# Scores of the RWKV key pair: masked copy on VectorE against a plain copy on ScalarE and a select on GpSimd

## The chip, the cores and the metric

The kernel runs on one core of a Trainium2 chip. The time is the device time of one execution in microseconds (us), and smaller is better. Engines carry the names of the profile: PE is TensorE (PEld its weight load), DVE VectorE, ACT ScalarE, POOL GpSimd, SP SyncE. A pair of an engine and a line, as DVE L542, means that engine's instructions of line 542 of the kernel before.

## The reference

A trunk of two layers over 256 tokens of width 1024. In each layer the normed input goes through one input projection into four token mixers (stick-breaking attention, RWKV-7 time mixing, MoBA attention, HGRN2 recurrence) and four gates; the gated sum of the four branches goes through an output projection, and an FFN of inner width 2816 follows. The part that matters here is RWKV's recurrence:

```python
def step(state, inp):
    r_t, w_t, k_t, v_t, a_t, b_t = inp
    sa = jnp.einsum('bhvk,bhk->bhv', state, a_t)
    state = (state * w_t[:, :, None, :] + sa[..., None] * b_t[:, :, None, :]
             + v_t[..., None] * k_t[:, :, None, :])
    return state, jnp.einsum('bhvk,bhk->bhv', state, r_t)
```

It runs over 256 steps in 4 heads of 64. A chunked form replaces the steps by products of matrices: for each chunk of 128 steps and each head there is a 128x128 score of every step s against every later step t, once for the pair (b, a) and (b, r), once for (k, a) and (k, r). Scores against a count where s < t, scores against r where s <= t, and all others are zero.

## The kernel before

All matrix products run on PE. A weight arrives as a raw tile of 128x1024 by a DMA on SP's queue, ACT rounds it into `hi` (L128) and DVE takes the rest as `lo = raw - hi` (L129); three matmuls then stand for one product (`mm3`). There are four buffers each for `raw`, `hi` and `lo`, and three PSUM buffers `pa` for projections. While PE works through projections, the mixers run as generators beside them: each `yield` names the latency that the generator's last work is thought to have, and `drive` goes on with it when the count of issued PE work has passed that. So the order in the program is set by PE work alone. From the program the tile framework then makes one instruction list for each engine, by its own estimates of when an operand is ready, and each engine works its list off in order; in the profile, instructions of one engine therefore need not stand in the order of the code.

In RWKV (`rwkv`, L465) the function `pair_scores` (L534) makes the scores of one chunk. It clears a tile `dst` of 128x4x256 by a memset on POOL, lets PE make the scores of four heads in two PSUM tiles of the tag `p1` (which has two buffers), and copies them to `dst` by two masked copies on DVE (L542); the mask `armask` holds s < t in its first 128 columns and s <= t in its last 128. It is called for each of two chunks with `bn` (the result is `LB`, L553) and for each of two chunks with `kh` (the result is `LK`, L568). `LB` is sent to DRAM by POOL (L548) and read back by ACT's queue (L564) as the 16x16 blocks `xb`; DVE inverts them in three levels of multiplications and sums (L591, L594) into `yb`, which goes to DRAM by POOL (L599) and back by ACT's queue (L602). `LK` is read by PE only at L735 and L766, in the last part of RWKV.

Other mixers run in the same stretch. MoBA's rotation shuffles q and k on DVE (L980), multiplies the shuffled part on DVE (L981), the other part on POOL (L982), and adds both on DVE (L983). Stick-breaking attention splits its result on ACT and DVE (`y` rows of L128 and L129). The second projection of HGRN2 leaves its two PSUM tiles `pa` by ACT (L810, L811), DVE (L812) and POOL (L813); the gate projection that comes after it needs these buffers.

Of the kernel before, what the change touches and what calls it, by code (L numbers as in the profile page):

```python
# [15 lines left out]
OP = mybir.AluOpType  # L16
# [30 lines left out]
def trunk(ctx, tc, x, w_t, w_n, w_br, w_out, w_gu, w_dn, par, lora, rows, gains, consts, masks, out):  # L47
    nc = tc.nc
# [8 lines left out]
    def sb(tag, width, dt=F32):  # L57
        return mx.tile([128, width], dt, name=tag, tag=tag, bufs=NB[tag])

    def ps(tag):  # L60
        return psum.tile([128, 512], F32, name=tag, tag=tag, bufs=NB[tag])

    def g2d(t, a):
        return t.rearrange("p (a t) -> p a t", a=a)
# [4 lines left out]
    def over(t, n):  # L69
        return t[:, None, :].to_broadcast([128, n, t.shape[-1]])  # L70
# [3 lines left out]
    def mm(o, l, r, start=True, stop=True):  # L74
        n = 1
        for d in r.shape[1:]:
            n *= d
        m = l.shape[-1]
        pe[0] += max(m / 1.2, n / 2.4) if r.dtype == F32R else max(m / 0.6, n / 0.6)
        nc.tensor.matmul(o, l, r, start=start, stop=stop)  # L80
# [114 lines left out]
    for i in range(20):  # L195
        nc.tensor.matmul(warm[:, 0:256], flat1[:, 0:128], flat1[:, 0:256], start=True, stop=True)  # L196
        if i in (8, 12):
            c = (i - 8) // 4
# [16 lines left out]
    armask = mk[:, 0:256]  # L215
# [220 lines left out]
    def head_sums(q, tag):  # L436
        p = ps(tag)
        for t in range(2):
            for hp in range(2):
                mm_cols(p[:, t * 4 + hp * 2:t * 4 + hp * 2 + 2], q[:, hp, t * 128:(t + 1) * 128], blk2)  # L440
        return p
# [4 lines left out]
    def hrow(a):  # L446
        return slice((a % 2) * 64, (a % 2) * 64 + 64)
# [17 lines left out]
    def rwkv(m, l, yT):  # L465
# [43 lines left out]
        p = head_sums(sq, "p1")  # L509
# [8 lines left out]
        p = ps("p1")  # L518
# [12 lines left out]
        yield 4500  # L531
        Y, LB, LK = [], [], []

        def pair_scores(src, dst, c):  # L534
            p = [ps("p1"), ps("p1")]
            nc.gpsimd.memset(dst, 0.0)
            for a in range(4):
                hp = a // 2
                mm(p[a % 2][:, hp * 256:(hp + 1) * 256], src[hrow(a), hp, c * 128:(c + 1) * 128],
                   AR[hrow(a), 2 * hp + c].rearrange("p u t -> p (u t)"))  # L540
            for u in range(2):
                nc.vector.copy_predicated(dst[:, u::2], over(armask, 2), g2d(p[u], 2))  # L542

        flat = dram.tile([8, 128 * 129], F32, name="flat")
        tri = dram.tile([64, 256], F32, name="tri")
# [5 lines left out]
        for c in range(2):  # L551
            LB.append(g2d(sb("b1", 1024), 4))
            pair_scores(bn, LB[c], c)  # L553
            yield 1600
            send(c)
# [4 lines left out]
        kh = g2d(sb("c1", 512), 2)  # L560
# [4 lines left out]
                                        ap=[[16 * 129, 64], [128, 16], [1, 16]]))  # L565
        for c in range(2):
            LK.append(g2d(sb("b1", 1024), 4))
            pair_scores(kh, LK[c], c)  # L568
            yield 3200
        nc.vector.tensor_copy(yb.rearrange("p s t -> p (s t)")[:, 1::34],  # L570
                              xb.rearrange("p s t -> p (s t)")[:, 1::34])
# [47 lines left out]
        for c in range(2):  # L619
            z5 = z[c].rearrange("p a (b u h) -> p a b u h", u=2, h=16)  # L620
            p = ps("p1")
# [4 lines left out]
        for c in range(2):  # L626
            p = ps("p1")
# [12 lines left out]
        p = [ps("p1"), ps("p1")]  # L640
# [6 lines left out]
        p = [ps("p1"), ps("p1")]  # L647
# [11 lines left out]
        for c in range(2):  # L659
            z6.append(g2d(sb("h1", 256), 4))  # L660
            p = ps("p1")
# [4 lines left out]
        for c in range(2):  # L666
            zs.append(g2d(sb("h1", 256), 4))
            p = ps("p1")
# [5 lines left out]
        for c in range(2):  # L674
            p = ps("p1")
# [6 lines left out]
        if l:  # L682
            p = ps("p1")
# [11 lines left out]
        p = ps("p1")  # L695
# [6 lines left out]
        p = ps("p1")  # L702
# [10 lines left out]
        p = head_sums(rx, "p1")  # L713
# [7 lines left out]
        p = ps("p1")  # L721
# [8 lines left out]
        for c in range(2):  # L730
            p = ps("p1")
# [9 lines left out]
            p = ps("p1")  # L741
# [3 lines left out]
            u = sb("h1", 256)  # L745
            nc.scalar.copy(u, p[:, 0:256])
            yield 1000
            if c == 0:
                p = ps("p1")
# [12 lines left out]
            p = ps("p1")  # L762
# [350 lines left out]
    def rwkv_s(m, l, yT):  # L1113
        yield from rwkv(m, l, yT)
# [181 lines left out]
```

## Time and profile before

| | us |
|---|---|
| median of 3 runs (924.91 to 926.95) | 926.62 |
| the profiled execution | 924.23 |
| its span, first to last instruction | 922.4 |
| PE busy | 905.6 |
| DVE busy | 650.8 |
| ACT busy | 475.4 |
| POOL busy | 88.2 |

The profile is of one execution. Times in its views count from the start of the span. A busy PE includes matmuls whose ends overlap. In the timeline an instruction's idle time before it, and what ended that, stand in brackets. The granted TensorE clock was 0.998 of full over the span.

### The profile page before, as it was taken

Reading aid. Unit: us, or ns where it says so; the run is one execution under the profiler, and the core shown is the slowest. Engines: PE = TensorE matmul, PEld = TensorE weight load, DVE = VectorE, ACT = ScalarE, POOL = GpSimd, SP = SyncE. Lnnn points to the kernel's source line nnn. Section 1 sums busy time; section 2 is a strip of 40 time slices with the busy share of each in tenths; the row PEclk is TensorE's granted clock in tenths of the full one; section 3 lists DMA queues with packets and bytes.
Section 4 is the critical chain, followed back from the end, with each engine's and each line's share of the span. In section 5 each row is a group of like instructions: output and inputs, shape, how many; then the busy total and the mean of one; then the engine's idle time right before and its main releaser. Section 6 shows DMA issues by size and latency. Waiting matters only on the chain.

```text
span 922.4 us, 15005 instructions
## 1 busy us (share of the span) xinstructions
PE 905.6 (98%) x5902; PEld 758.9 (82%) x5902; DVE 650.8 (71%) x957; ACT 475.4 (52%) x726; POOL 88.2 (10%) x100
## 2 busy tenths in 40 slices
PE   8999999999999999999999999999999999999996
PEld 5999777778788888888889987777788888888885
DVE  6667877887766666668567778768778566666665
ACT  6564385345635445556355646644455445545453
POOL 3012100323000000000000211033130000000000
PEclk9999999999999999999999999999999999999999
DMA  8644453435754565567434544533377356556551
GB/s 311 221 149 152 121 174 126 135 131 184 257 199 140 181 198 189 183 208 268 141 116 160 163 138 152 174 104 117 116 218 256 106 188 207 191 182 192 183 183 46
DMA packets 48536, 158.11 MB, mean 171 GB/s; under 512 B 9393, under 2 KB 9777, under 8 KB 48466
## 3 DMA queue, kind: packets, MB, share of 16 engines
q1 hardware_dynamic: 43632, 155.19, 51.6%
q10 hardware_dynamic: 4450, 0.79, 0.5%
q0 software_dynamic: 384, 1.18, 0.4%
q8 instruction: 46, 0.75, 0.3%
q14 instruction: 24, 0.20, 0.1%
HBM read 154.91 MB, written 2.23 MB: 170 GB/s over the span
## 4 chain that ended last, share of the span: by engine, by line
PE 84%; DVE 9%; issue 2%; ACT 2%; DMA 1%; POOL 1%; ACTq 0%; POOLq 0%; DVEq 0%
PE pa L80 58%; PE p L80 23%; DVE lo L129 2%; PE pa L89 1%; PE p L89 1%; DVE b L542 1%; ACT hi L128 1%; DMA flat<-b 1%; DVE b L867 1%; DVE b L965 1%; DMA raw<-in_w_out_dram 1%; PE pa L196 0%; DVE xy L591 0%; DVE c L981 0%; DVE c L980 0%
## 5 line engine op out<-in xcount | busy, mean ns | idle before, releaser
L129 DVE TENSOR_TENSOR lo<-raw,hi 128x1024 fp32r<-128x1024 f32 x268 | 330.9, 1240 | 154.5 <-ACT hi L128 150.9
L128 ACT CAST hi<-raw 128x1024 fp32r<-128x1024 f32 x268 | 279.3, 1049 | 234.3 <-PE pa L80 109.3
L80 PE MATMUL pa<-h,hi 128*128 128x256 f32 (+1 forms) x1280 | 278.0, 339 | 0.0
L80 PEld LDWEIGHTS pa<-h,hi 128*128 128x128 f32 x1280 | 216.1, 190 | 24.5 <-issue 2.0
L80 PE MATMUL pa<-hi,h 128*128 128x512 f32 x576 | 193.2, 400 | 3.1 <-DVE p L812 3.1
L80 PE MATMUL pa<-h,lo 128*128 128x256 f32 x960 | 180.1, 283 | 0.0
L80 PEld LDWEIGHTS pa<-h,lo 128*128 128x128 f32 x960 | 148.8, 191 | 6.9 <-issue 0.7
L80 PEld LDWEIGHTS pa<-hi,h 128*128 128x128 f32 x576 | 108.2, 188 | 29.6 <-DVE p L812 4.0
L80 PE MATMUL p<-hi,c 128*128 128x512 f32 (+1 forms) x352 | 113.5, 394 | 0.0
L80 PE MATMUL pa<-lo,h 128*128 128x512 f32 x288 | 112.9, 392 | 0.0
L80 PEld LDWEIGHTS p<-hi,c 128*128 128x128 f32 x352 | 66.1, 189 | 15.1 <-DVE c L129 0.6
L80 PE MATMUL p<-lo,c 128*128 128x512 f32 (+1 forms) x176 | 69.3, 394 | 0.0
L80 PEld LDWEIGHTS pa<-lo,h 128*128 128x128 f32 x288 | 54.2, 188 | 9.6
L263 POOL TENSOR_TENSOR rs<-rs,half 128x1 f32<-128x1 f32 x10 | 5.9, 594 | 471.4 <-DVE rs L262 471.4
L80 PE MATMUL pa<-hi,y 128*128 128x512 f32 x128 | 44.0, 399 | 0.1
L80 PE MATMUL p<-hi,b 128*128 128x512 f32 x128 | 41.6, 396 | 0.3 <-DVE b L129 0.2
L80 PEld LDWEIGHTS p<-lo,c 128*128 128x128 f32 x176 | 33.2, 189 | 6.7
L1033 POOL TENSOR_TENSOR p<-p,gt 128x512 f32<-128x512 f32 x16 | 30.9, 1950 | 39.4 <-DVE gt L1031 31.9
L340 DVE TENSOR_TENSOR gt<-gt,pa 128x256 f32<-128x256 f32 x80 | 33.1, 413 | 0.0
L128 ACT CAST c<-xy 128x512 fp32r<-128x512 f32 x20 | 12.4, 620 | 39.7 <-DVE xy L1136 39.7
L80 PEld LDWEIGHTS pa<-hi,y 128*128 128x128 f32 x128 | 24.0, 188 | 6.7 <-issue 0.7
L339 ACT COPY gt<-pa 128x256 f32<-128x256 f32 x80 | 29.1, 364 | 0.0
(278 smaller groups left out, 941.6 us busy)
## 6 DMA issues: line engine op xcount, KB each, us to landing
raw<-in_w_gu_dram SPq DMA_DIRECT2D x88, 512.0 KB, 3.9
raw<-in_w_n_dram SPq DMA_DIRECT2D x80, 512.0 KB, 3.6
raw<-in_w_dn_dram SPq DMA_DIRECT2D x44, 512.0 KB, 3.5
raw<-in_w_t_dram SPq DMA_DIRECT2D x40, 512.0 KB, 3.5
raw<-in_w_br_dram SPq DMA_DIRECT2D x16, 512.0 KB, 3.7
raw<-in_w_out_dram SPq DMA_DIRECT2D x16, 512.0 KB, 4.3
b<-in_gains_dram SPq DMA_DIRECT2D x4, 512.0 KB, 5.5
flat<-b POOLq DMA_DIRECT2D x4, 256.0 KB, 3.3
```

What stands on the lines that cost most here:

```text
L80: nc.tensor.matmul(o, l, r, start=start, stop=stop)
L89: nc.tensor.transpose(o, i, ident)
L128: a = nc.scalar.copy(dst[0], src)
L129: return a, (eng or nc.vector).tensor_tensor(dst[1], src, dst[0], op=OP.subtract)
L263: nc.gpsimd.tensor_tensor(dst, dst, half[:, :dst.shape[-1]], op=OP.pow)
L339: nc.scalar.copy(dst, p[:, 256:512])
L340: nc.vector.tensor_tensor(dst, dst, p[:, 0:256], op=OP.add)
L542: nc.vector.copy_predicated(dst[:, u::2], over(armask, 2), g2d(p[u], 2))
L867: nc.vector.tensor_tensor(qv, qv, t4[s, :, :, 0:1].to_broadcast([64, 2, 2 * nb, hb]), op=OP.mult)
L965: nc.vector.tensor_tensor_scan(kb, kb, reset[t][:, ::-1], 1.0, op0=OP.mult, op1=OP.add)
L1033: e.tensor_tensor(mg[f, t], mg[f, t], g, op=OP.add)
```

## The change

`pair_scores` gets a switch, which the two calls for `LK` set. With it the memset on POOL and the two masked copies on DVE are left out. Two plain copies on ACT take the scores from the two PSUM tiles, each 128 partitions by 2 heads by 256, and two selects on POOL work in place on the result: each takes 128 columns of all four heads and writes zero where t - s + u - 1 is negative (u = 0 for the columns against a, u = 1 for those against r). The calls for `LB` stay as they are.

```diff
-        def pair_scores(src, dst, c):
+        def pair_scores(src, dst, c, select=False):
             p = [ps("p1"), ps("p1")]
-            nc.gpsimd.memset(dst, 0.0)
+            if not select:
+                nc.gpsimd.memset(dst, 0.0)
...
             for u in range(2):
-                nc.vector.copy_predicated(dst[:, u::2], over(armask, 2), g2d(p[u], 2))
+                if select:
+                    nc.scalar.copy(dst[:, u::2], g2d(p[u], 2))
+                else:
+                    nc.vector.copy_predicated(dst[:, u::2], over(armask, 2), g2d(p[u], 2))
+            for u in range(2 if select else 0):
+                v = dst[:, :, u * 128:(u + 1) * 128]
+                nc.gpsimd.affine_select(v, v, [[0, 4], [1, 128]], OP.is_ge, 0.0, base=u - 1, channel_multiplier=-1)
...
             LK.append(g2d(sb("b1", 1024), 4))
-            pair_scores(kh, LK[c], c)
+            pair_scores(kh, LK[c], c, True)
```

## Rows read from the trace of the kernel before

**Rows 1.** The page's first part: busy us, share of the span, instructions.
```profile
PE 905.6 (98%) x5902; PEld 758.9 (82%) x5902; DVE 650.8 (71%) x957; ACT 475.4 (52%) x726; POOL 88.2 (10%) x100
```

**Rows 2.** Waits of PE: engine, line, releaser: us in total, times, longest.
```profile
PE pa L80 <- DVE p L812: 3.1, 2, 1.6
```

**Rows 3.** Timeline of PE around both waits: start, us, instruction, idle before it.
```profile
110.20 0.50 PE L80 MATMUL pa<-hi,h 128*128 128x512 f32 x1 [1.57 <-DVE p L812]
...
561.74 0.50 PE L80 MATMUL pa<-hi,h 128*128 128x512 f32 x1 [1.56 <-DVE p L812]
```

**Rows 4.** Timeline of DVE, 94 to 110 us (layer 0).
```profile
94.45 1.21 DVE L129 TENSOR_TENSOR lo<-raw,hi 128x1024 fp32r<-128x1024 f32 x1
...
96.22 0.74 DVE L980 STREAM_SHUFFLE c<-p 128x512 f32<-128x512 f32 x1
96.86 1.36 DVE L542 COPY_PREDICATED b<-mk,p 128x512 f32<-128x512 uint8 x2
98.12 0.98 DVE L981 TENSOR_TENSOR c<-c,cn 128x512 f32<-128x512 f32 x1
99.03 0.68 DVE L129 TENSOR_TENSOR y<-p,y 128x512 fp32r<-128x512 f32 x1
99.63 0.68 DVE L983 TENSOR_TENSOR c<-c,p 128x512 f32<-128x512 f32 x1
100.22 0.68 DVE L981 TENSOR_TENSOR c<-c,cn 128x512 f32<-128x512 f32 x1
100.83 0.25 DVE L591 TENSOR_TENSOR xy<-h,yb 64x64 f32<-64x64 f32 x1
...
101.87 1.20 DVE L129 TENSOR_TENSOR lo<-raw,hi 128x1024 fp32r<-128x1024 f32 x1
103.00 1.03 DVE L591 TENSOR_TENSOR xy<-yb,h 64x512 f32<-64x512 f32 x1
103.97 1.33 DVE L542 COPY_PREDICATED b<-mk,p 128x512 f32<-128x512 uint8 x2
105.20 0.66 DVE L594 TENSOR_REDUCE h<-xy 64x64 f32<-64x512 f32 x1
...
109.74 0.40 DVE L812 TENSOR_TENSOR p<-p,pa 128x256 f32<-128x256 f32 x1
```

**Rows 5.** Timeline of DVE in layer 1: the second masked copy there.
```profile
555.50 1.35 DVE L542 COPY_PREDICATED b<-mk,p 128x512 f32<-128x512 uint8 x2
```

**Rows 6.** Timeline of PE: the scores of both chunks of LK.
```profile
92.48 1.14 PE L80 MATMUL p<-b,c 64*128 64x256 f32 x8
...
98.92 1.14 PE L80 MATMUL p<-b,c 64*128 64x256 f32 x8
```

**Rows 7.** Timeline of ACT, 92 to 106 us.
```profile
92.34 1.06 ACT L938 COPY c<-p 128x512 f32<-128x512 f32 x2
93.30 0.61 ACT L801 ACTIVATE p<-pa 128x512 f32<-128x512 f32 x1
94.72 0.59 ACT L128 CAST y<-p 128x512 fp32r<-128x512 f32 x1 [0.82 <-PE p L80]
96.99 1.06 ACT L128 CAST hi<-raw 128x1024 fp32r<-128x1024 f32 x1 [1.68 <-DVE c L980]
100.98 1.05 ACT L128 CAST hi<-raw 128x1024 fp32r<-128x1024 f32 x1 [2.94 <-PE pa L80]
```

**Rows 8.** POOL's groups by shape: busy us, mean ns of one, idle before.
```profile
L1033 POOL TENSOR_TENSOR p<-p,gt 128x512 f32<-128x512 f32 x16 | 30.9, 1950 | 39.4 <-DVE gt L1031 31.9 <-DVE bs L715 7.6
...
L982 POOL TENSOR_TENSOR p<-p,cn 128x512 f32<-128x512 f32 x4 | 4.3, 1091 | 18.3 <-DVE c L980 18.3
...
L238 POOL MEMSET reset<- 128x512 f32 x2 | 1.0, 517 | 0.0
```

**Rows 9.** Timeline of POOL: memsets of LB and LK, MoBA's products, inverse's DMA.
```profile
68.50 3.63 POOL L536 MEMSET b<- 128x1024 f32 x4
...
96.41 2.15 POOL L982 TENSOR_TENSOR p<-p,cn 128x512 f32<-128x512 f32 x2 [9.16 <-DVE c L980]
108.98 0.58 POOL L599 DMA_DIRECT2D tri<-yb  x1 [10.43 <-DVE yb L594]
```

**Rows 10.** Timeline of DVE: one shape beside POOL's L720 and alone, 168 to 177 us.
```profile
170.63 1.41 DVE L868 TENSOR_TENSOR c<-c,tot 128x256 f32<-128x256 f32 x1
...
176.57 0.41 DVE L868 TENSOR_TENSOR c<-c,tot 128x256 f32<-128x256 f32 x1
```

## The prediction

> **What bounds the kernel now.** I read the busy shares first. PE is busy for 905.6 of 922.4 us [rows 1], so only some 17 us of PE's idle time can be won at all, and an edit on DVE, ACT or POOL counts only where PE stands still for it. So the second view is the list of what PE's matmuls waited for. Its largest entry is two waits, 3.1 us together, for DVE's L812 [rows 2]. The timeline of PE puts them at 110.20 us in layer 0 (1.57 us) and at 561.74 us in layer 1 (1.56 us) [rows 3]: the same place in both layers, where the gate projection wants a PSUM buffer `pa` that HGRN2's L812 still reads.
>
> The third view says why L812 is late. DVE works without a pause from 94.45 us on; L812 starts at 109.74 us as the last of that queue [rows 4]. The masked copies of LK stand in it twice, at 96.86 and 103.97 us, both ahead of L812 [rows 4]. So in this stretch DVE sets the time, and the reader should see that the changed instructions sit in the one queue that PE waits for. The order of that queue is the framework's: L591, which comes after `pair_scores` in the code, already runs ahead of the second masked copies [rows 4].
>
> The profiled execution took 924.23 us, 1.83 more than its span and 2.4 below the median of 926.62. I work in the profile's times and add the difference to the median at the end. Less than 0.2%, 1.85 us, can't be told from no change.
>
> **What goes.** On DVE two masked copies go per chunk. A row of two lasts 1.36 or 1.33 us, but the next instruction starts 1.26 us (98.12 - 96.86) and 1.23 us (105.20 - 103.97) after it began [rows 4], so the queue loses 2.5 us ahead of L812 in layer 0. Layer 1 has the same [rows 5]. The two memsets per layer are 0.91 us each (3.63 / 4) at about 70 us, on a POOL that is then idle until far later [rows 9]; they hide behind all else and their going is worth nothing.
>
> If nothing came back, L812 would start 2.5 us sooner and the wait of 1.57 would vanish in both layers: 3.1 us.
>
> **What comes on ACT.** Two copies per chunk of 128x512 from PSUM; the nearest row is L938, the same shape from PSUM, two in 1.06 us [rows 7]. Chunk 0's scores end at 93.62 us, when ACT is at L801 until 93.91, so the copies fill 93.9 to 95.0 and push the `y` split from 94.72 to 95.0 [rows 6, 7]. The next `hi` starts at 96.99, after 1.68 us of idle time that covers the 0.3 us. Chunk 1's scores end at 100.06, and ACT waits until 100.98 for its next `hi` [rows 6, 7]; the copies can delay that by about 0.2 us (100.06 + 1.06 = 101.1). Its `lo` runs on DVE only after 106 us. So I cost the ACT copies at nothing; bounds are 0 and, if every us of them stood ahead of L812, 2.1 us per layer. No gain can come from more work on ACT itself.
>
> **What comes on POOL.** Four selects per layer of 128x512, in place. No select is in the trace. Below stands the memset of the same size, 0.517 us, which reads nothing; above, the product of two tensors, 1.09 us in L982 and 1.95 us as the mean of L1033, which has the same shape [rows 8]. A select reads one tensor, so I take 0.8 us, between the memset and the nearer of the products, and keep 0.52 and 1.95 for the range. The cost for PE is not POOL's own time (POOL is idle from 98.56 to 108.98 us [rows 9]) but what it does to DVE.
>
> **DVE and POOL in each other's way.** L868, two inputs in SBUF, takes 1.41 us beside POOL's work and 0.41 us alone [rows 10]. L981 takes 0.98 us where POOL's L982 still runs until 98.56, and 0.68 where it does not [rows 4, 9]. So a POOL instruction that reads SBUF stops a DVE instruction with two SBUF operands for most of its length. [...] In this stretch most of DVE's queue is of that kind: `lo`, L981, L983, L591. The masked copies are not hit: a mask in SBUF, data in PSUM, 0.68 us each beside L982.
>
> Chunk 0, with selects of 0.8 us. They are ready at 95.0, but `lo` holds DVE until 95.6. Selects 95.6 to 97.2; L981 would start at 96.86 and waits to 97.2, then 0.6 to 97.8; L982's first product 97.8 to 98.9 (2.15 / 2 = 1.07); L983 needs it: 98.9 to 99.5; L982's second 99.5 to 100.55; the second L981 to 101.15, L591 0.2, L983 0.6, a sum at L594 0.25: 102.2. Before, this point was 101.87 [rows 4]. So where 1.26 us were taken out, the queue is 0.3 us later: the masked copies had been running beside L982, and without them DVE meets L982 and the selects head on. If POOL runs L982 ahead of the selects, they fall among L983, L981 and L591, and the delay is up to 1.2 us (both 0.8 us paid in full, 0.9 for L982, 0.3 that before paid already, less 1.26). With selects of 0.52 us the point is 101.65, 0.2 us sooner.
>
> Chunk 1. Selects about 102.2 to 104, against `lo` and L591. If both stop DVE, 1.6 us come back for 1.23 saved: 0.4 later. If one falls beside the sum L594 (0.66 us, one input), 0.8 comes back: 0.4 sooner. I take the middle, 0.0.
>
> Sum per layer: -2.5 us of masked copies, +1.55 us in chunk 0 (1.26 + 0.3), +1.2 us in chunk 1, and so L812 0.2 us later; two layers, 0.4 us. That is 924.6 us on the profile's scale and 927.0 on the median's: no change that can be measured. Where the stall stays, PE's 1.57 us wait stays with it.
>
> [...]
>
> **The rivals.** *The selects get out of DVE's way* (faster): they are near 0.5 us and land beside shuffles, sums and PSUM reads. For it: POOL is idle for 10 us after L982 [rows 9], and DVE has such instructions between. Against it: `lo` and L591 alternate without a pause. L812 then moves by 1.6 us or more, both waits go, 3.1 us: 923.5. An earlier `yb` also lets the DMA of L599 go sooner, which ACT waits for; perhaps 0.4 us more.
>
> *POOL paces the stretch* (slower): one mechanism, DVE's in-order queue standing at L983, L981 and `lo` while POOL works selects and L982 one after the other. With 1.1 us per select, chunk 0 ends at 102.8 (+0.9) and chunk 1 costs 2.2 - 1.23 = 1.0 more: 1.9 per layer, 3.8 in all: 930.4. At 1.95 us it is 5.2 per layer, 10.5 in all: 937. It decides from about 0.95 us per select on, where the loss passes 1.85 us. For it: L1033's 1.95 us [rows 8] shows how long a product lasts in contention. Against it: one operand instead of two.
>
> *The queues come out in another order* (the change does not act as drawn): the framework lays the lists out anew. If ACT's copies of chunk 1 stood ahead of the `hi` at 96.99, that would start at 101.1 and its `lo` at 102.2 instead of 101.87: 0.3 us per layer, 927.3 if L812 moves by no more than that.
>
> **How the numbers follow.** No measurable change 0.40; selects out of the way 0.31; POOL paces 0.25; another order 0.04, of which half ends above 1.85 us. That makes faster 0.31, same 0.42, slower 0.27. The likeliest case's own range is 924.8 to 928.5. The range for 8 in 10 reaches to both waits gone, 923.4, and to selects of about 1.0 us, 929.8.
>
> **What would show it.** In the trace after: four ACT copies of about 0.53 us and four selects per layer; the duration of one select against 0.8; L981, L983, `lo` and L591 lengthened beside them; where L812 starts against 109.74, and PE's wait ahead of the gate projection against 1.57. I am wrong if that wait is gone in both layers or more than twice as long, and most of all if a select stops no DVE instruction.

## The result and the profile after

The changed kernel takes 933.25 us (median of 4 runs, 932.21 to 934.24), the kernel before, timed beside it, 926.79 (924.91 to 927.78). The ratio is 1.0073, 95% interval [1.0057, 1.0089]: slower by some 6.5 us where no measurable change was forecast, and above the forecast range, which ended at 929.8.

| us | before | after |
|---|---|---|
| profiled execution | 924.23 | 932.21 |
| its span | 922.4 | 930.5 |
| PE busy | 905.6 | 910.7 |
| DVE busy | 650.8 | 650.1 |
| PE's wait ahead of the gate projection, layer 0 / 1 | 1.57 / 1.56 | 3.67 / 3.57 |

All stands at the place that the prediction named. Where [rows 2, 3] had two waits of 1.6 us, the waits of PE (us in total, times, longest) and its timeline show two of 3.6 us, for the same evacuation, the instruction that empties a PSUM buffer. Line numbers go with each run's own kernel: DVE L812 of before is L819 here and L815, L819, L822 or L829 in later runs.

```profile
PE pa L80 <- DVE p L819: 7.2, 2, 3.7
```
```profile
115.17 0.68 PE L80 MATMUL pa<-hi,h 128*128 128x512 f32 x1 [3.67 <-DVE p L819]
...
568.78 0.50 PE L80 MATMUL pa<-hi,h 128*128 128x512 f32 x1 [3.57 <-DVE p L819]
```

Times in this trace first have to be shifted. Its first matmuls run at about half the pace of before: L199's four take 3.78 us after, 2.18 before (the granted clock reads 1.00 in both from 4 to 8 us). By the scores of LK this trace is 2.86 us late at chunk 0 (92.48 in [rows 6], 95.34 after) and 2.87 at chunk 1 (98.92 and 101.79), and PE has not stood still for the change by then.

PE at the scores of both chunks after:
```profile
95.34 1.13 PE L80 MATMUL p<-b,c 64*128 64x256 f32 x8
...
101.79 1.13 PE L80 MATMUL p<-b,c 64*128 64x256 f32 x8
```

PE's start after:
```profile
4.41 3.78 PE L199 MATMUL p<-b,h 1*128 1x512 f32 x4
8.12 1.67 PE L196 MATMUL pa<-h 128*128 128x256 bf16 x7
```
PE's start before:
```profile
4.34 2.18 PE L199 MATMUL p<-b,h 1*128 1x512 f32 x4
6.45 0.94 PE L196 MATMUL pa<-h 128*128 128x256 bf16 x7
```

Now DVE's queue after, against [rows 4]:

```profile
99.69 2.68 DVE L988 TENSOR_TENSOR c<-c,cn 128x512 f32<-128x512 f32 x2
102.30 1.12 DVE L990 TENSOR_TENSOR c<-c,p 128x512 f32<-128x512 f32 x1
103.34 0.68 DVE L129 TENSOR_TENSOR y<-p,y 128x512 fp32r<-128x512 f32 x1
...
104.73 0.33 DVE L601 TENSOR_REDUCE yb<-xy 64x16 f32<-64x64 f32 x2
105.09 1.06 DVE L598 TENSOR_TENSOR xy<-yb,h 64x512 f32<-64x512 f32 x1
...
108.98 0.68 DVE L601 TENSOR_REDUCE yb<-xy 64x64 f32<-64x512 f32 x1
109.59 1.21 DVE L129 TENSOR_TENSOR lo<-raw,hi 128x1024 fp32r<-128x1024 f32 x1
113.56 1.23 DVE L129 TENSOR_TENSOR lo<-raw,hi 128x1024 fp32r<-128x1024 f32 x1 [2.77 <-ACT hi L128]
114.70 0.41 DVE L819 TENSOR_TENSOR p<-p,pa 128x256 f32<-128x256 f32 x1
```

The reader is to see two things. The inverse is done earlier: `yb` is ready at 109.66, and POOL sends it at 109.96. Less the shift of 2.87 that is 107.09, where it was 108.98 before [rows 9]: 1.9 us sooner. But DVE, which had no pause before, then stands 2.77 us for ACT's `hi`. So the view of ACT comes next (ACTq is its sequencer, which issues a DMA):

```profile
96.61 1.08 ACT L544 COPY b<-p 128x512 f32<-128x512 f32 x2
...
99.85 1.06 ACT L128 CAST hi<-raw 128x1024 fp32r<-128x1024 f32 x1 [1.67 <-PE pa L80]
102.95 1.08 ACT L544 COPY b<-p 128x512 f32<-128x512 f32 x2 [2.04 <-PE p L80]
103.91 1.06 ACT L128 CAST hi<-raw 128x1024 fp32r<-128x1024 f32 x1
111.95 0.41 ACTq L609 DMA_DIRECT2D h<-tri  x1
112.48 1.04 ACT L128 CAST hi<-raw 128x1024 fp32r<-128x1024 f32 x1 [7.51 <-DMA tri<-yb]
113.43 0.37 ACT L817 COPY p<-pa 128x256 f32<-128x256 f32 x1
113.69 0.39 ACT L818 ACTIVATE p<-pa 128x256 f32<-128x256 f32 x1
```

The same stretch of ACT before:

```profile
103.72 1.06 ACT L128 CAST hi<-raw 128x1024 fp32r<-128x1024 f32 x1 [1.68 <-PE pa L80]
105.07 0.37 ACT L810 COPY p<-pa 128x256 f32<-128x256 f32 x1 [0.30 <-PE pa L80]
105.34 0.39 ACT L811 ACTIVATE p<-pa 128x256 f32<-128x256 f32 x1
112.79 0.41 ACTq L602 DMA_DIRECT2D h<-tri  x1
113.25 0.37 ACT L810 COPY p<-pa 128x256 f32<-128x256 f32 x1 [7.52 <-DMA tri<-yb]
```

Before, the DMA of L602, which reads back what L599 wrote and so waits for it, stood in ACT's list behind the evacuation L810, L811 that PE needs, ahead of the second one only. After (L609), it stands ahead of both evacuations and of one `hi`. In neither trace does ACT start anything that stands behind this DMA in its list ahead of it (7.52 us of idle time there before, 7.51 after), so all of them now wait 7.5 us for a DMA that has nothing to do with them. L818 ends at 114.08, L819 follows one `lo` later, and PE goes on at 115.17.

Behind the wait PE's granted clock is lower. The windows after PE's wait give length, busy us (and instructions) of PE, PEld, DVE, ACT and POOL, granted clock, DMA share and GB/s; first after, then before:

```profile
116.00:118.00 2.00, 2.00 (x6) 1.54 (x5) 2.00 (x6) 0.44 (x1) 0.52 (x1) 0.50 0.58 229
118.00:120.00 2.00, 2.00 (x8) 1.59 (x8) 2.00 (x3) 1.99 (x7) 1.56 (x2) 0.81 0.00 0
120.00:122.00 2.00, 2.00 (x11) 1.63 (x10) 1.97 (x5) 2.00 (x6) 0.00 (x0) 1.00 0.56 133
```
```profile
112.00:114.00 2.00, 2.00 (x11) 1.65 (x10) 0.06 (x1) 0.75 (x3) 0.00 (x0) 1.00 0.66 232
114.00:116.00 2.00, 2.00 (x11) 1.65 (x10) 1.49 (x2) 1.98 (x2) 1.56 (x2) 1.00 0.30 28
```

After 3.67 us of idle time the granted clock is 0.50 from 116 to 118 us, and six matmuls fit in 2 us where eleven did. After before's 1.57 us it stayed at 1.00. (The length of the wait alone doesn't decide it; see the last section.)

The span grew by 8.1 us: 2.87 at the start, 2.1 and 2.0 in the two waits, and about 1.1 net elsewhere; the lower clock is a part of that, and no run prices it by itself. The start is no part of the change: the profiled execution of the kernel before with four selects added (below) has it too, that of the changed kernel with its DMA moved once (below) does not. L199's four take 3.78 us in 8 of the 13 profiles of this case, half of them of kernels built on the one before. Without it the profiles differ by 5.2 us, near the lower end of the interval for the times (0.57% of 926.8 is 5.3 us).

### The profile page after: what moved, and what is told of

It is laid out like the page before. It is cut to its first block, busy times and chain, and to the rows that moved or that the text cites. A ratio compares the mean times of both kernels' runs of the same rounds, so it can differ in the third digit from the quotient of the medians.

```text
span 930.5 us, 15012 instructions
## 1 busy us (share of the span) xinstructions
PE 910.7 (98%) x5902; PEld 762.8 (82%) x5902; DVE 650.1 (70%) x949; ACT 479.6 (52%) x734; POOL 93.5 (10%) x104
## 4 chain that ended last, share of the span: by engine, by line
PE 86%; DVE 7%; issue 3%; POOL 1%; DMA 1%; ACT 1%; ACTq 0%; POOLq 0%; DVEq 0%
PE pa L80 60%; PE p L80 23%; DVE lo L129 2%; PE pa L89 1%; PE p L89 1%; DVE b L874 1%; DVE b L972 1%; PE pa L196 0%; POOL p L989 0%; POOL b L549 0%; DMA tri<-yb 0%; DMA raw<-in_w_t_dram 0%; PE p L199 0%; DMA flat<-b 0%; DVE xr L411 0%
## 5 line engine op out<-in xcount | busy, mean ns | idle before, releaser
L80 PE MATMUL pa<-hi,h 128*128 128x512 f32 x576 | 195.4, 404 | 7.2 <-DVE p L819 7.2
```

## The experiments

Theory A: the DMA of L609 at its new place on ACT makes the loss. Rival B: the selects on POOL do, through what they do to DVE (the prediction's "POOL paces"). `cb` is the tile that this DMA fills with the inverse. The kernel before is timed anew beside each group of runs, and each time is compared with the one of its group.

**Put the DMA behind the first evacuation again** (`left` collects the two Sigmoid activations of L818; `issue_after` puts an instruction behind the named one in the list):

```diff
-            nc.scalar.activation(gs[:, t], p[:, 256:512], AF.Sigmoid)
+            left.append(nc.scalar.activation(gs[:, t], p[:, 256:512], AF.Sigmoid))
...
-        nc.scalar.dma_start(cb, ...)
+        with tc.issue_after(left[0].ins):
+            nc.scalar.dma_start(cb, ...)
```

> The changed kernel with one thing more: ACT's DMA that reads the inverse back (cb) is queued behind the first evacuation of HGRN2's pa (the activation of the t = 0 half), as it stood in the kernel before. All other lists are as in the changed kernel. Theory A (the change moved that DMA, which waits for the inverse, ahead of the evacuation on ACT's in-order queue, and PE waits for the pa buffer): PE's wait ahead of the gate projection falls from 3.7 and 3.6 us to 0.5 to 1.0 us in each layer; by the DVE list L812's counterpart then comes 1.1 us after the lo at 109.6, about 0.8 us after PE wants the buffer. Time 924 to 926.5, at or below the kernel before. Rival B (selects on POOL stop DVE and make it late): the wait stays at 3 us or more and the time at 932 to 934.

928.11 us against 927.09, ratio 1.0017 [1.0004, 1.0030]. So 5 of the 6.5 us come back, with all copies and selects still in place; A had expected 924 to 926.5, which was too good. The waits of PE fell to 0.99 and 0.86 us, below before's, but a new one appeared in each layer (1.52 and 1.09 us), in its timeline:

```profile
109.88 0.50 PE L80 MATMUL pa<-hi,h 128*128 128x512 f32 x1 [0.99 <-DVE p L822]
...
118.72 0.50 PE L80 MATMUL pa<-lo,h 128*128 128x512 f32 x1 [1.52 <-DVE lo L129]
```

and the DVE timeline of this kernel says where it is from: DVE's list now has L616, which uses what that DMA brings, ahead of a `lo`.

```profile
115.30 0.69 DVE L616 TENSOR_TENSOR xy<-h,mk 128x512 f32<-128x512 f32 x1 [4.09 <-DMA h<-tri]
...
116.91 1.75 DVE L129 TENSOR_TENSOR lo<-raw,hi 128x1024 fp32r<-128x1024 f32 x1
```

It is the same fault one engine on: an instruction that waits for a DMA stands ahead of work that PE needs.

**The change without its selects** (the copies become an activation with scale 0; the key scores are left out of the computation):

```diff
-                    nc.scalar.copy(dst[:, u::2], g2d(p[u], 2))
+                    nc.scalar.activation(dst[:, u::2], g2d(p[u], 2), AF.Copy, scale=0.0)
...
-            for u in range(2 if select else 0):
+            for u in range(0):
```

> The changed kernel without the four selects per layer; so that nothing unmasked is used, ACT writes the key pair's scores times zero (this leaves the key scores out of the result). ACT's list still has the DMA of cb ahead of the evacuation. Theory A: PE's wait ahead of the gate projection stays at 2.5 to 3.7 us in each layer and the time at 930 to 933.5. Rival B (selects stop DVE): the wait goes to under 1 us and the time to 924 to 926.

931.81 against 927.09, 1.0054 [1.0042, 1.0067]. Three quarters of the loss (some 5 us) stay without a single select, and so do PE's waits:

```profile
114.44 0.50 PE L80 MATMUL pa<-hi,h 128*128 128x512 f32 x1 [3.02 <-DVE p L819]
...
567.70 0.50 PE L80 MATMUL pa<-hi,h 128*128 128x512 f32 x1 [3.21 <-DVE p L819]
```

B falls as the main cause. This run also settles whom DVE meets in chunk 0. In its DVE timeline the two products L988 take as long as in the changed kernel (2.68 us), where only POOL's L989 can be in the way, while the sum L990 is back at 0.68 from 1.12:

```profile
99.42 2.69 DVE L988 TENSOR_TENSOR c<-c,cn 128x512 f32<-128x512 f32 x2
102.03 0.68 DVE L990 TENSOR_TENSOR c<-c,p 128x512 f32<-128x512 f32 x1
```

**The kernel before with the selects added** (behind its masked copies, where they change no value):

```diff
             pair_scores(kh, LK[c], c)
+            for u in range(2):
+                v = LK[c][:, :, u * 128:(u + 1) * 128]
+                nc.gpsimd.affine_select(v, v, [[0, 4], [1, 128]], OP.is_ge, 0.0, base=u - 1, channel_multiplier=-1)
```

> The kernel before with the four selects per layer added on POOL behind DVE's masked copies (they change nothing in the data). ACT's list is that of the kernel before. Theory A: the selects cost what they stop DVE for, 0 to 1 us per layer, so the wait ahead of the gate projection is 1.5 to 2.5 us and the time 926.5 to 929. Rival B: the wait grows by 2 us per layer as in the changed kernel, 3.5 us or more, time 930 or more.

928.94 against 927.09, 1.0018 [1.0005, 1.0031]: 1.7 us (0.5 to 2.9) for four selects in each of two layers. PE's waits at the gate projection grew by 0.57 and 0.60 us (to 2.14 and 2.16). So the selects do hold DVE up, by about 0.6 us per layer, a fifth or so of what the change lost. Here they run beside other DVE instructions than in the changed kernel, so their price there can differ.

**The kernel before with that DMA on POOL's queue** (`nc.scalar.dma_start(cb, ...)` becomes `nc.gpsimd.dma_start(cb, ...)`):

> The kernel before with the DMA that reads the inverse back issued by POOL's queue in place of ACT's. Theory A: in the kernel before the first evacuation already stood ahead of that DMA, and DVE's queue set PE's wait; so the wait stays at 1.5 us in both layers, and only what ACT did behind the DMA comes sooner: 925.5 to 927, no change or half a us less. If ACT's DMA wait also made the loss of the kernel before, the wait of 1.57 us would go and the time would be 923.5.

927.48 against 927.09, 1.0003 [0.9991, 1.0016]: no change. The waits fell to 1.38 and 1.21 us, but new ones of 1.60 and 1.49 for a `lo` came, behind DVE's L606 (L616 in the run above is the same product), at which DVE stood 4.15 us for the DMA. ACT being free is not enough.

**The DMA behind both evacuations, in the changed kernel** (as the first, with `left[1]`):

> The changed kernel with the DMA of cb queued on ACT behind both evacuations of HGRN2's pa (in the run before only behind the first); the framework then puts it, and on DVE the products that need cb, some entries later. Theory A (in-order lists that wait for the inverse's way through DRAM are the whole loss, beyond what the selects stop on DVE): PE's wait ahead of the gate projection stays near 0.9 us and the wait of 1.1 to 1.5 us for a lo, which came from DVE standing at the product with cb, goes; time 924.5 to 926.5, below the kernel before by some 1 us. Rival B: what is left is the selects' doing, so the time stays at 928.

922.98 against 926.49, 0.9957 [0.9946, 0.9969]. This version of the change is faster than before, by 3.5 us of medians or 4.0 by the ratio, more than A expected (924.5 to 926.5). At this place PE waits 0.60 and 0.82 us, and no more for a `lo`:

```profile
112.07 0.50 PE L80 MATMUL pa<-hi,h 128*128 128x512 f32 x1 [0.60 <-DVE p L822]
...
561.35 0.50 PE L80 MATMUL pa<-hi,h 128*128 128x512 f32 x1 [0.82 <-DVE p L822]
```

On ACT both evacuations (L820) run before the DMA, and on DVE the product L616 stands at 119.88, behind what PE needs:

```profile
107.91 0.37 ACT L820 COPY p<-pa 128x256 f32<-128x256 f32 x1 [0.30 <-PE pa L80]
...
110.14 0.37 ACT L820 COPY p<-pa 128x256 f32<-128x256 f32 x1 [1.57 <-PE pa L80]
...
115.10 0.43 ACTq L611 DMA_DIRECT2D h<-tri  x1
```

The granted clock is 1.00 in the windows from 112 to 116 us behind that wait.

**The kernel before with the DMA ahead of both evacuations** (the loss without copies or selects; the generator's `yield`s are moved behind the DMA, and L810 is put behind it):

```diff
-            yield 3200
+            yield 3200 - 3200 * c
...
-        yield 4000
...
-        yield 2500
-        nc.scalar.dma_start(cb, ...)
-        yield 2500
+        trig.append(nc.scalar.dma_start(cb, ...))
+        yield 12200
...
-            nc.scalar.copy(iv[:, t], p[:, 0:256])
+            with tc.issue_after(trig[-1].ins):
+                nc.scalar.copy(iv[:, t], p[:, 0:256])
```

> The kernel before, masked copies on DVE and no selects, with only ACT's list changed the way the change did it: the DMA of cb stands ahead of both evacuations of pa (the latencies named by three yields are moved behind it, so that PE's order stays the same). Theory A: PE's wait ahead of the gate projection grows from 1.57 to 4 to 6 us in both layers and the time is 931 to 937, as slow as the changed kernel or slower. Rival B (the loss needs the selects or the copies): wait 2 us or less, time 926 to 928.

931.86 against 926.49, 1.0046 [1.0028, 1.0064]. The time is as theory A has it, the place isn't: ACT stood 4.63 us for the DMA instead of 7.5, and PE's wait at the gate projection was 1.34 and 1.30 us, which is what rival B had for it. The loss came as waits for `lo` of 1.29 and 2.39 us, behind a product on DVE that stood 3.98 us for the DMA. So the order of the lists alone, with no instruction of the change, can cost 4.3 us by the ratio or 5.4 by the medians, most of what the change lost. But this edit moved more than one instruction and stops PE at another place, so it shows what instructions behind a DMA wait cost and is no copy of the change's path.

**The kernel before with the DMA behind both evacuations** (the first diff with `left[1]`):

> The kernel before (masked copies on DVE, no selects) with the DMA of cb queued on ACT behind both evacuations of pa, as in the run of the changed kernel with that order. Question: does the order alone make the gain of 3.9 us, or the change together with the order? Theory A (the change gives DVE 2.5 us per layer back less what the selects stop): without the change L812 stays late, PE's wait ahead of the gate projection stays at 1.4 to 1.6 us in both layers, and only later waits on ACT and DVE go: 924.5 to 926.5. Theory C (the gain is the order's alone): 922.5 to 923.5.

925.63 against 926.83, 0.9994 [0.9981, 1.0007]: no change that can be told, with waits of 1.69 and 1.32 us. With DVE's queue as full as before, L812 (L815 here) is late although ACT is free: the second evacuation on ACT (L813) is done by 110.81, and PE waits for L815 until 113.46.

```profile
110.44 0.37 ACT L813 COPY p<-pa 128x256 f32<-128x256 f32 x1 [1.58 <-PE pa L80]
```
```profile
113.46 0.50 PE L80 MATMUL pa<-hi,h 128*128 128x512 f32 x1 [1.69 <-DVE p L815]
```

**The same order with neither mask nor select** (the changed kernel, DMA behind both, scale 0 and no selects; the key scores are left out):

> The changed kernel with the DMA of cb behind both evacuations and without the selects; ACT writes the key scores times zero, which leaves them out of the result. Against the same kernel with selects (wait 0.6 to 0.8 us, 923.0 us) this prices the selects where no list is blocked: theory A says 0 to 0.8 us per layer, wait 0 to 0.3 us, time 921.5 to 923. If selects stopped DVE for their full 0.9 us each, 2 us per layer would come back: 920.

920.39 against 926.83, 0.9945 [0.9923, 0.9966], waits 0.34 and 0.60 us. The time lies below A's range and near the rival's 920, the waits say otherwise: against the ordered change with selects they fell by 0.26 and 0.22 us only. By the medians of both runs, each against its own kernel before, the selects cost 2.9 us, by the ratios (0.9957 and 0.9945) 1.1, within the noise of both. Part of that is the start: this profile began at the fast pace (L199's four, here L200, in 2.33 us), that of the ordered change at the slow one (3.78). At the scores of chunk 0, first with selects, then without, the traces are 2.34 us apart:

```profile
95.31 1.13 PE L80 MATMUL p<-b,c 64*128 64x256 f32 x8
```
```profile
92.97 1.13 PE L80 MATMUL p<-b,c 64*128 64x256 f32 x8
```

From there to the end the two spans (921.5 and 918.6) differ by 0.6 us. So the selects' price in this order isn't settled between 0.6 and 2.9 us.

**A second order: a `lo` behind the evacuation.** DVE's list has one `lo` ahead of L812 that PE needs only later. In the kernel before it is put behind (the third weight's split after L812 of t = 0):

```diff
+            e = nc.vector.tensor_tensor(gs[:, t], gs[:, t], p[:, 256:512], op=OP.mult)
+            if t == 0:
+                late[:] = [e.ins, 2]
...
+        elif late and late[1] == 0:
+            with tc.issue_after(late[0]):
+                split(w, raw)
```

> The kernel before with one lo on DVE (third weight of the gate projection) queued behind L812 in place of ahead of it. DVE's list alone sets PE's 1.57 us wait there, so it should fall by that lo's 1.13 us, to about 0.45 us in both layers; time 924 to 925.5, about 2 us below the kernel before. If another queue set L812, the wait would stay at 1.5.

925.32 against 926.49, 0.9989 [0.9974, 1.0004]: not told from no change, where 2 us were expected. The waits fell to 0.52 and 0.27 us, but `lo` ones of 0.69 and 0.54 came. Both orders together in the kernel before:

> The kernel before with both orders mended (the DMA of cb behind both evacuations on ACT, the third gate lo behind the evacuation on DVE). Theory A: PE's wait ahead of the gate projection 0.3 to 0.5 us, time 923 to 925: within 2 us of the changed kernel with both orders (922.8), above it by 0 to 1.5 us. Theory C: 922 to 923, the same as that kernel, so that the change itself is worth nothing.

928.40 against 926.83, 1.0013 [0.9995, 1.0031]: the expected gain is missing. The waits at the gate projection are 0.43 and 0.19, but the delayed `lo` costs 2.28 and 2.48, because L616 stood 4.15 us for its DMA ahead of it on DVE. And both in the changed kernel:

> The changed kernel with both orders mended: the DMA of cb behind both evacuations on ACT, and the third gate lo behind the evacuation on DVE. Theory A: then the masked copies' 2.5 us on DVE are a gain, PE's wait ahead of the gate projection is 0 to 0.3 us, time 923.5 to 925.5, below the kernel before by 2 to 3 us and no more than 1 us from the kernel before with its lo moved. Rival B (selects' contention makes DVE as late as the masked copies did): wait 0.5 to 1 us, time 926 or more.

922.76 against 926.49, 0.9954 [0.9937, 0.9970]: as good as with the one order, no better. No wait of PE at the gate projection is left, and `lo` waits of 0.21 and 0.28 us are there.

## Why the prediction was wrong

**Right: where the time is decided.** Both waits of [rows 3] moved, and what the change cost came through them; "more than twice as long" (3.67 against 1.57) was named as what would make the forecast wrong.

**Chunk 0: the number right, partly by luck.** Forecast: the point after the sum at 102.2 against 101.87 before. Measured 105.09 less 2.87, 102.22. But the forecast had both selects ahead of POOL's products; POOL ran the products L989 (L982 of before) first, from 99.24, and the selects from 101.78. That is the order for which the prediction gave a delay of up to 1.2 us, and it came to 0.35. The reason was half right: DVE meets L989 head on (2.68 us for two products against 0.98 + 0.68), and the run without selects shows that L989 alone does it. Of the two selects, one shows in L990 (1.12 against 0.68).

**Nearly right: a select's price.** 0.89 us as the mean of eight (POOL's group: busy us, mean ns, idle), for 0.8 assumed; 0.67 each in chunk 1, where of DVE's work only the last 0.25 us of a `lo` ran beside them, and 1.07 each around L990:

```profile
L549 POOL TENSOR_SCALAR_AFFINE_SELECT b<-b 128x512 f32<-128x512 f32 x8 | 6.9, 888 | 0.0
```
```profile
101.78 2.14 POOL L549 TENSOR_SCALAR_AFFINE_SELECT b<-b 128x512 f32<-128x512 f32 x2
...
109.96 0.59 POOL L606 DMA_DIRECT2D tri<-yb  x1 [6.04 <-DVE yb L601]
110.55 1.34 POOL L549 TENSOR_SCALAR_AFFINE_SELECT b<-b 128x512 f32<-128x512 f32 x2
```

**DVE and POOL in each other's way: right, but it goes both ways.** The prediction priced chunk 1 by what the selects take from DVE. In the ordered change (the first two fences below: POOL, then DVE) the two selects of chunk 1 took 2.47 us beside two `lo`, where they took 1.34 in the changed kernel, and the `lo` took 2.34, where two later ones with POOL idle took 2.36. There POOL's instructions got longer and DVE's didn't. The forecast for chunk 0 has the selects wait for a `lo` in this way (95.6 for 95.0). No timeline among its rows shows that direction, and no run shows it of a select in chunk 0 (in the changed kernel POOL ran the products first, and its selects there met no `lo`); the trace of before shows it of a product (the last two: POOL, then DVE): L1033 took 2.28 us beside a `lo` of 1.21, L717 of the same shape, with no `lo` beside it until its end, 1.05. And [rows 10] names the wrong neighbour: L720 ended at 170.32, and what ran beside L868 at 170.63 was POOL's L1033 (170.28 to 171.76); the reading of the two durations stays.

```profile
110.30 2.47 POOL L550 TENSOR_SCALAR_AFFINE_SELECT b<-b 128x512 f32<-128x512 f32 x2
```
```profile
109.34 2.34 DVE L129 TENSOR_TENSOR lo<-raw,hi 128x1024 fp32r<-128x1024 f32 x2
...
117.60 2.36 DVE L129 TENSOR_TENSOR lo<-raw,hi 128x1024 fp32r<-128x1024 f32 x2
```
```profile
164.37 2.28 POOL L1033 TENSOR_TENSOR p<-p,gt 128x512 f32<-128x512 f32 x1 [7.59 <-DVE bs L715]
166.61 1.05 POOL L717 TENSOR_TENSOR c<-c,bs 128x512 f32<-128x512 f32 x1
```
```profile
164.28 1.21 DVE L129 TENSOR_TENSOR lo<-raw,hi 128x1024 fp32r<-128x1024 f32 x1
```

**Wrong: chunk 1.** Its selects were put at 102.2 to 104, against `lo` and L591, and priced at 1.2 us of the 1.23 saved. They ran at 110.55, behind POOL's DMA L606, when `yb` was done. So the saving of 1.23 stayed, and one `lo` that had stood ahead of the end of `yb` (1.13 us) now stands behind it; less chunk 0's 0.35 that makes 2.0, and the shifted 107.09 shows 1.9 us sooner.

**The step that failed: "The queues come out in another order", 0.3 us per layer, chance 0.04.** The prediction kept all lists as before, except that it asked where the ACT copies would stand against a `hi`. It knew that the framework lays the lists out by its own estimates of readiness, and that an earlier `yb` sends an earlier DMA; it counted that as "perhaps 0.4 us more" of gain. It didn't ask where the issue of the read-back would then stand in ACT's list. It moved ahead of both evacuations, and PE got its buffer not 0.3 us but 2.0 to 2.1 us per layer later (waits of 3.67 and 3.57 us for 1.57 and 1.56). The 7.5 us for which ACT stands at this DMA were there in the trace of before, past the 106 us at which [rows 7] end; what they cost depended on which instructions stood behind. Moving that one issue back gives 5 of 6.5 us, further back all of it and 3.5 to 4.0 us more.

That the moved place makes the loss, all but what the selects cost (1.8 us by the ratios with and without them, 1.0073 and 1.0054), is shown by these two runs and by the one without selects. That the framework moved it because it took `yb` to be ready sooner is my reading of the two orders; no run showed its estimates.

**Also wrong: "What comes on ACT" at nothing.** The copies are as forecast (two in 1.08 us), and the two `hi` around them start where they did before (96.98 and 101.04 by the shift, against 96.99 and 100.98). But ACT wasn't followed past 106 us.

**The first estimate: its direction held, its size and its place did not.** With nothing given back the prediction had 3.1 us of gain, the two waits. The run that comes nearest to that, ordered and without selects, gained 5.1 us by the ratio and still had waits of 0.34 and 0.60. The ordered change gained 3.5 to 4.0 with the selects in; that this is close to 3.1 is chance, for the waits shrank by 0.97 and 0.74 us only. In layer 0 its trace is 2.83 us late at the scores of chunk 0 (95.31 against 92.48 in [rows 6]) and 0.83 late at the products of 126.38 (125.55 before), so 2.0 us are won in that stretch: 0.97 in PE's wait, 0.42 in a `lo` wait of before that is gone, and 0.6 that no single wait shows. The order alone gave 0.9994 in the kernel before, so the gain needs the change and the order together. Why the second order brought nothing there (1.0013, not told from no change) is seen in the trace (L616 ahead of `lo`), but no run with L616 moved was made.

## What to carry to other kernels

Where a framework makes the in-order lists, relief of one engine can also re-sort the lists of the others, as it did here: ask of every issue in the stretch that waits for another DMA which instructions would stand behind it if it came earlier, and price them by the wait that the trace of before already has there. When a wait names a releaser that itself stood idle, go on to what released that one: PE named DVE, DVE named ACT, and ACT named the DMA. If a sound change loses, compare the lists of both kernels before the durations, and fix the one order that moved, behind everything that the bounding engine needs.

## What the runs showed of the hardware

A select of 128x512 f32 in place on POOL took 0.67 us with DVE nearly idle and 1.07 around DVE's sum of two SBUF operands, which itself went from 0.68 to 1.12 (both in the changed kernel), and 1.24 (2.47 for two) beside two `lo`, which it didn't lengthen (2.34 us beside selects, 2.36 with POOL idle, both in the ordered change).

After 3.67 us without matmuls PE's granted clock was 0.50 from 116 to 118 us and 0.81 from 118 to 120; after 0.60 us in the ordered change and 1.57 in the kernel before it stayed at 1.00. The length of a wait alone doesn't tell. In the run without selects single matmuls of 128x512 went from 0.39 to 0.63 us after 3.02 us in layer 0 (mean granted clock 0.95 from 96 to 130 us) and stayed at 0.39 after 3.21 us in layer 1 (1.00 from 545 to 590 us). In the kernel before with the DMA ahead of both evacuations they went from 0.39 to 0.63 after 2.39 us in layer 1. What else decides is not shown here.

The pace of PE's first matmuls differs between profiles whose programs start alike: L199's four took 2.18 us in one and 3.78 in another, at a granted clock that reads 1.00 in both, and the trace was 2.9 us longer for it. So profiles that differ by less are to be aligned at a mark behind the start first.
